# The first stage of a one-core transformer block in a fixed order, with half the first modulation sums and each second row's product moved to TensorE

## The chip, the cores and the metric

The kernel runs on one core of one Trainium2 chip. A core has TensorE (PE; its weight loads are listed as PEld), VectorE (DVE), ScalarE (ACT), GpSimd (POOL) and SyncE (SP), which here only issues transfers. Each engine executes its own list of instructions in order. The metric is the device time of one execution in microseconds (us). One execution was also recorded by the hardware profiler; all rows of the trace come from that one.

## The reference

One decoder block on 1024 tokens of width 1024, batch 1, all in float32. Only its head matters here:

```python
mod = einsum('bd,de->be', silu(c), w_ada) + b_ada            # w_ada: 1024 x 6144
shift1, scale1, gate1, shift2, scale2, gate2 = split(mod, 6)
h = rms_norm(x, norm1_w) * (1 + scale1) + shift1
proj = einsum('btd,de->bte', h, w_in)                        # w_in: 1024 x 7184
q, k, v, r, a_lr, su, sv, g_a, g_b = split(proj, ...)
```

From `proj` come a chunked gated linear attention (its decay from `a_lr`, rank 16), a spatial gating unit, two sigmoid gates and one output projection; after that a mixer that picks 16 of 16384 single-neuron experts for each of 8 heads and token, and a final norm.

## The kernel before

The tokens are done in two halves of 512. In a half the normed and modulated input is kept transposed: row k (of 8) holds 128 features by 512 tokens. To keep float32 accuracy at TensorE's quicker rate, each operand is split into a rounded part and its rest (`hTh`, `hTl` for the input, `wh`, `wl` for a weight tile), and three products are summed: high by high, high by rest, rest by high. A *group* is one 1024x512 slice of `w_in`: 8 rows, and for each row four blocks of 128 tokens, so 12 products into four PSUM tiles `mm`. The weight tiles `wt` (128x512, four buffers) are loaded by SP; ScalarE rounds them (L1253), VectorE takes the rest (L1254). The 14 groups, the output projection and the query projection follow one another.

The *first stage* is what must happen before and during the first group (`G_V0`) of the first half:

- `x_first`: eight loads of x, squares on ScalarE (L1196), pair sums on VectorE (L1198), a product with `ones` (L1199), the norm of each token `rstd`, and its spread over the partitions by a product (L1165) into `rrow` (L1167).
- `ada_cols(kp)`, four times: a quarter of the columns of shift1 and scale1. Each of 8 rows of `w_ada` (a tile 128x512, two rows to a buffer, eight buffers) is scaled by a column of silu(c) and added up, in two chains of four rows: the first by ScalarE (L1124), three by VectorE (L1126). Eight one-column products with `ones` (L1132) add up the partitions, VectorE adds the bias into `mod` (L1134) and makes `scol` = (1 + scale) * norm weight (L1136). A quarter serves two rows k.
- `h_first(k)`: `xt` times `rrow` on VectorE (L1224); the modulated row twice on ScalarE, rounded into `hTh` (L1211) and whole into `xt` (L1213); the rest `hTl` on VectorE (L1216).
- after the group, 24 products of 16 rows (`gaux`) for the decay input `a_lr`, with `walr_h` and `walr_l`.

The text issues these in the order of the program, and a list scheduler that simulates a timeline reorders each engine's list; only places under `issue_after` are held. Later, queues of generators interleave other work with the groups: the remaining rows of `w_ada` (L1103 to L1108, four rows of 1024 columns), the routing and the gathered experts, all of whose order the scheduler also sets.

## Time and profile before

| | |
|---|---|
| median of 3 runs | 1452.01 us (1451.76 to 1453.45) |
| the profiled execution | 1450.17 us, span 1448.4 us |
| mean granted TensorE clock | 0.971 |
| TensorE busy | 1348.1 us, 93% of the span |
| VectorE busy | 1091.7 us, 75% |
| ScalarE busy | 737.9 us, 51% |
| DMA, mean | 238 GB/s |

The span is the time from the profile's first event to its last; the execution's own time is 1.8 us more. In a row of the timeline the first number is the start in us, the second the length, then engine, line, operation, result<-operands; a number behind x says how many neighbours were merged. A row of the groups gives the count, the busy time with the mean length in ns, and the idle time before it with what ended it. An f32 product with f32 on both sides leaves two records in the trace, and each record of TensorE is longer than the spacing to the next one, since products overlap.

### The profile page before, as it was taken

To read this page: it belongs to the slowest core of one execution; us is meant where nothing else is said; L and a number is where in the kernel's file an instruction comes from. 1 tells how busy PE (TensorE), PEld (TensorE's weight loads), DVE (VectorE), ACT (ScalarE), POOL (GpSimd) and SP (SyncE) were. 2 spreads that over 40 slices of the span, in tenths; PEclk is the share of its full clock that TensorE was granted. 3 is DMA by queue.
4 is the path that set the end of the run, shared out by engine and by line. 5 is a ranking of instruction groups with operands and counts; after the bars stand their busy time and mean duration, and the time that the engine had idled before them with its cause. 6 is when DMAs were issued, how large, how long until landed. Compare 5 with 4: busy or idle time off the path is not lost.

```text
span 1448.4 us, 19642 instructions
## 1 busy us (share of the span) xinstructions
PE 1348.1 (93%) x6004; PEld 1039.6 (72%) x6004; DVE 1091.7 (75%) x3114; ACT 737.9 (51%) x1611; POOL 278.7 (19%) x275
## 2 busy tenths in 40 slices
PE   3999999999999889997989999999988999789996
PEld 2778877888888778776868787887766886445553
DVE  6584768443468669988879888778889877799775
ACT  4454333333255456474534677556645555556542
POOL 0100001000000011422442133221111024443331
PEclk8899999999999999998999999999998999999999
DMA  9552454322258484757587689796687669987984
GB/s 321 184 214 95 170 184 161 105 95 88 88 171 280 160 291 168 265 177 275 194 308 263 222 325 343 286 354 216 219 324 264 227 216 356 355 347 303 419 331 166
DMA packets 120836, 345.00 MB, mean 238 GB/s; under 512 B 15033, under 2 KB 24505, under 8 KB 108690
## 3 DMA queue, kind: packets, MB, share of 16 engines
q0 software_dynamic: 32064, 165.95, 30.7%
q1 hardware_dynamic: 70992, 133.20, 26.8%
q10 hardware_dynamic: 17666, 44.53, 8.5%
q8 instruction: 48, 0.79, 0.2%
q14 instruction: 66, 0.54, 0.1%
HBM read 319.40 MB, written 24.23 MB: 237 GB/s over the span
## 4 chain that ended last, share of the span: by engine, by line
PE 41%; DMA 8%; DVE 7%; issue 5%; ACT 4%; POOL 1%; ACTq 0%; DVEq 0%; POOLq 0%
PE acc L606 7%; PE mm L181 6%; PE mm L182 6%; PE mm L184 6%; DMA uv<-in_tab_dram,ix 4%; PE mm L187 3%; PE mm L188 3%; PE mm L189 3%; PE aux L1655 2%; PE hps L578 1%; DMA wt<-in_w_inp_dram 1%; PE hps L579 1%; DVE wl L1254 1%; DVE uv L580 1%; DMA xb<-in_x_dram 1%
## 5 line engine op out<-in xcount | busy, mean ns | idle before, releaser
L1253 ACT ACTIVATE wh<-wt 128x512 fp32r<-128x512 f32 x368 | 228.2, 628 | 322.9 <-PE mm L182 133.5
L1254 DVE TENSOR_TENSOR wl<-wt,wh 128x512 fp32r<-128x512 f32 x368 | 247.7, 685 | 137.1 <-ACT wh L1253 73.2
L181 PE MATMUL mm<-wh,hTh 128*128 128x512 f32 x672 | 265.9, 398 | 3.1 <-ACT wh L1253 3.1
L182 PE MATMUL mm<-wh,hTl 128*128 128x512 f32 x672 | 263.8, 395 | 0.0
L184 PE MATMUL mm<-wl,hTh 128*128 128x512 f32 x672 | 207.6, 394 | 0.0
L181 PEld LDWEIGHTS mm<-wh,hTh 128*128 128x128 f32 x672 | 127.1, 189 | 35.0 <-ACT wh L1253 4.8
L182 PEld LDWEIGHTS mm<-wh,hTl 128*128 128x128 f32 x672 | 126.9, 189 | 27.1 <-issue 1.0
L184 PEld LDWEIGHTS mm<-wl,hTh 128*128 128x128 f32 x672 | 125.6, 188 | 27.0 <-DVE wl L1254 0.6
L525 POOL DMA_INDIRECT uv<-in_tab_dram,ix x74 | 80.4, 1086 | 262.9 <-ACT ix L557 178.3
L187 PE MATMUL mm<-wh,hTh 128*128 128x512 f32 x224 | 90.5, 413 | 8.4 <-ACT hTh L1211 5.5
L182 PE MATMUL mm<-hTl,wh 128*128 128x512 f32 x240 | 96.5, 402 | 0.0
L181 PE MATMUL mm<-hTh,wh 128*128 128x512 f32 x240 | 95.9, 400 | 0.0
L580 DVE SCALAR_TENSOR_TENSOR uv<-uv,hps 128x512 f32<-128x512 f32 x112 | 74.8, 679 | 24.5 <-DMA uv<-in_tab_dram,ix 16.8
L188 PE MATMUL mm<-wl,hTh 128*128 128x512 f32 x224 | 89.1, 398 | 0.1
L189 PE MATMUL mm<-wh,hTl 128*128 128x512 f32 x224 | 88.4, 397 | 0.0
L187 PE MATMUL mm<-hTh,wh 128*128 128x256 f32 (+1 forms) x208 | 71.6, 346 | 10.7 <-DVE q L1383 7.6
L188 PE MATMUL mm<-hTl,wh 128*128 128x256 f32 (+1 forms) x208 | 69.8, 337 | 3.0 <-DVE hTl L173 3.0
L184 PE MATMUL mm<-hTh,wl 128*128 128x512 f32 x240 | 71.4, 398 | 0.0
L752 POOL DMA_INDIRECT uvd<-in_down_dram,dix x32 | 37.1, 1159 | 177.8 <-DVE cidx L353 40.0
L618 DVE SCALAR_TENSOR_TENSOR vl<-uv,r,vh 128x512 fp32r<-128x512 f32 x84 | 61.3, 745 | 10.6 <-ACT vh L617 7.7
L189 PE MATMUL mm<-hTh,wl 128*128 128x256 f32 (+1 forms) x208 | 68.9, 337 | 0.0
L578 PE MATMUL hps<-hh,E 128*128 128x512 f32 x132 | 62.4, 473 | 4.5 <-DVE uv L580 3.6
(938 smaller groups left out, 2875.3 us busy)
## 6 DMA issues: line engine op xcount, KB each, us to landing
wt<-in_w_inp_dram SPq DMA_DIRECT2D x224, 256.0 KB, 3.5
wt<-in_w_qp_dram SPq DMA_DIRECT2D x80, 256.0 KB, 3.0
wada<-in_w_ada_dram SPq DMA_DIRECT2D x32, 512.0 KB, 4.8
wt<-in_w_outp_dram SPq DMA_DIRECT2D x64, 256.0 KB, 3.5
wada<-in_w_ada_dram SPq DMA_DIRECT2D x32, 256.0 KB, 5.8
s_d<-so ACTq DMA_DIRECT2D x28, 256.0 KB, 5.3
xr<-in_x_dram ACTq DMA_DIRECT2D x8, 512.0 KB, 6.5
x_d<-x ACTq DMA_DIRECT2D x8, 512.0 KB, 4.4
```

The source lines that it names most:

```text
L181: nc.tensor.matmul(ps, lh, rh, start=False, stop=False)
L182: nc.tensor.matmul(ps, *((lh, rl) if feat else (ll, rh)), start=False, stop=False)
L184: nc.tensor.matmul(ps, *((ll, rh) if feat else (lh, rl)), start=False, stop=False)
L187: nc.tensor.matmul(ps, lh, rh, start=first, stop=False)
L188: nc.tensor.matmul(ps, lh, rl, start=False, stop=False)
L189: return nc.tensor.matmul(ps, ll, rh, start=False, stop=last).ins
L525: nc.gpsimd.indirect_dma_start(out=dst[:], out_offset=None, in_=src, in_offset=off)
L578: nc.tensor.matmul(hps, Ej, hh[:, sl], start=True, stop=False)
L580: nc.vector.scalar_tensor_tensor(uv[0][:, sl], uv[0][:, sl], 1.0, hps, op0=OP.mult, op1=OP.mult, accum_out=r[:, 2 + n:3 + n])
L606: ins = nc.tensor.matmul(acc[:, sl], W, v[:, sl], start=first, stop=last).ins
L1253: nc.scalar.activation(wh, wt, AF.Identity)
L1254: nc.vector.tensor_tensor(wl, wt, wh.bitcast(F32), op=OP.subtract)
```

## The change

The first stage gets a function of its own, `first_group`, whose instructions go out through `put`: each is held behind the one that the same engine issued before it, so the order of the text is the order on each engine.

- Squares are added up one by one on VectorE into one tile; four one-column products give the row sums. Five products of 256 columns, with no use for the result (`warm`), stand between the squares on TensorE.
- Of the first quarter of the modulation, rows 1, 3, 5 and 7 of `w_ada` (`DIRECT`) no longer go through the chain: TensorE multiplies them with the column of silu(c) itself, four one-column products a row. The other quarters have one chain of 8 rows, not two of four: 1 step on ScalarE and 7 on VectorE, and four closing products, not eight.
- `xt` times `rrow` is done two rows at a time, when a quarter comes up, not eight rows ahead.
- Rows 1, 3, 5 and 7 of the group are multiplied whole, in f32 (`whole`): four products, no `wh` and `wl`. The even rows keep the split form. `hTl` is still made for all, for the decay products, which now stand between the rows of the group.
- The loads of `walr`, `wal`, `balt`, `keyst` and `sgub` go from ScalarE's queue to SP's: `walr` behind the first two weight tiles, the others at the end of the stage.
- `weights_ahead` holds its splits behind the last modulation (`hlast`), and the second half's rows are modulated on VectorE as before.

The diff, cut to its core:

```diff
-HA = (range(8), ())
+DIRECT = ((1, 3, 5, 7), (), (), ())
+WARM = (2, 3, 4, 5, 6)
...
-        for src, hi, lo in ((walr, walr_h, walr_l), (wal, wal_h, wal_l)):
-            nc.vector.tensor_copy(hi, src)
-            nc.vector.tensor_tensor(lo, src, hi.bitcast(F32), op=OP.subtract)
+        tail = {}
+
+        def put(eng, fn, *args, **kw):
+            with tc.issue_after(tail[eng]) if eng in tail else nullcontext():
+                tail[eng] = getattr(getattr(nc, eng), fn)(*args, **kw).ins
+
+        def split_const(src, hi, lo):
+            put("vector", "tensor_copy", hi, src)
+            put("vector", "tensor_tensor", lo, src, hi.bitcast(F32), op=OP.subtract)
...
-        def ada_cols(kp):
...
+        class AdaCols:
+            def __init__(self, kp):
+                w2 = 2 * P
+                self.kp, self.direct = kp, DIRECT[kp]
+                self.acc = gl.tile([P, 2, w2], F32, name="adc", bufs=3)
...
+            def add(self, n):
+                for _ in range(n):
+                    q = self.chain.pop(0)
+                    if len(self.chain) + len(self.direct) == KD - 1:
+                        put("scalar", "activation", self.acc, self.wa[q], AF.Identity, scale=sc[:, q:q + 1])
                     else:
+                        put("vector", "scalar_tensor_tensor", self.acc, self.wa[q], sc[:, q:q + 1], self.acc,
+                            op0=OP.mult, op1=OP.add)
...
+            def product(self, src, rhs, first, last):
+                for c in range(2):
+                    for j in range(2):
+                        put("tensor", "matmul", self.ps[:, c, j:j + 1], src[:, c, j * P:(j + 1) * P], rhs,
+                            start=first and c == 0 and j == 0, stop=last and c == 1 and j == 1)
+
+            def products(self, qs):
+                for q in qs:
+                    self.product(self.wa[q], sc[:, q:q + 1], q == self.direct[0], False)
+
+            def close(self):
+                self.product(self.acc, ones[:, 0:1], not self.direct, True)
+
+            def store(self):
+                k = 2 * self.kp
+                put("vector", "tensor_tensor", mod.rearrange("p (c k) -> p c k", c=2)[:, :, k:k + 2], self.ps,
+                    badat.rearrange("p (c k) -> p c k", c=2)[:, :, k:k + 2], op=OP.add)
+                put("vector", "scalar_tensor_tensor", scol[:, k:k + 2], mod[:, KD + k:KD + k + 2], 1.0, n1t[:, k:k + 2],
+                    op0=OP.add, op1=OP.mult)
...
-        def x_first():
...
+        def first_group(src, evac, aps):
...
+            def fetch(kp):
+                st = AdaCols(kp)
+                for k in (2 * kp, 2 * kp + 1):
+                    wts[k] = wst_p.tile([P, 512], F32, name="wt")
+                    put("sync", "dma_start", wts[k], src[:, k, :])
+                return st
...
+            st = fetch(0)
+            put("sync", "dma_start", walr, w_alr)
+            acc = t2("sqa")
+            warm = gauxt([P, 256])
+            for k in range(KD):
+                sq = rowp.tile([P, HALF], F32, name="sq", tag="row") if k else acc
+                put("scalar", "activation", sq, xts[k], AF.Square)
+                if k in WARM:
+                    put("tensor", "matmul", warm, ones, sq[:, 0:256], start=True, stop=True)
+                if k:
+                    put("vector", "tensor_tensor", acc, acc, sq, op=OP.add)
+            sps = auxt([P, BH])
...
+                put("tensor", "matmul", sps[:, i:i + 1], acc[:, i * P:(i + 1) * P], ones[:, 0:1], start=i == 0,
+                    stop=i == BH - 1)
+            st.products(st.direct[:2])
+            st.add(2)
+            rstd = sm_p.tile([P, BH], F32, name="rstd")
...
+            st.add(1)
+            dg = t2("dg")
...
+            st.products(st.direct[2:])
+            rps = auxt([P, HALF])
+            put("tensor", "matmul", rps, ones, dg, start=True, stop=True)
+            rrow = t2("rrow")
+            put("scalar", "activation", rrow, rps, AF.Identity)
+            st.add(len(st.chain))
+            st.close()
+
+            def products(k, wh, wl):
+                for n in range(3):
+                    a, w = ((hTh, wh), (hTh, wl), (hTl, wh))[n]
+                    for i, cs in enumerate(cuts):
+                        put("tensor", "matmul", pss[i], a[:, k, cs], w, start=k == 0 and n == 0, stop=False)
+
+            def whole(k):
+                for i, cs in enumerate(cuts):
+                    put("tensor", "matmul", pss[i], xts[k][:, cs], wts[k], start=False, stop=k == KD - 1)
+
+            def low(k):
+                wh = wsp.tile([P, 512], F32R, name="wh")
+                wl = wsp.tile([P, 512], F32R, name="wl")
+                put("scalar", "activation", wh, wts[k], AF.Identity)
+                put("vector", "tensor_tensor", wl, wts[k], wh.bitcast(F32), op=OP.subtract)
+                return wh, wl
+
+            def scale_row(k):
+                put("vector", "tensor_tensor", xts[k], xts[k], rrow, op=OP.mult)
+
+            def modulate(dst, k):
+                put("scalar", "activation", dst, xts[k], AF.Identity, scale=scol[:, k:k + 1], bias=mod[:, k:k + 1])
+
+            def rest_of(k):
+                put("vector", "tensor_tensor", hTl[:, k], xts[k], hTh[:, k].bitcast(F32), op=OP.subtract)
+
+            def alpha(k):
+                for n, (a, w) in enumerate(((hTh, walr_h), (hTl, walr_h), (hTh, walr_l))):
+                    put("tensor", "matmul", aps, w[:, k], a[:, k], start=k == 0 and n == 0, stop=k == KD - 1 and n == 2)
+
+            whl = low(0)
+            scale_row(0)
+            for ka in range(0, KD, 2):
+                kb = ka + 1
+                st.store()
+                scale_row(kb)
+                st = fetch(kb // 2 + 1) if kb < KD - 1 else None
+                more = st.add if st else id
+                more(1)
+                for k in (ka, kb):
+                    modulate(hTh[:, k], k)
+                    modulate(xts[k], k)
+                for k in (ka, kb):
+                    more(1)
+                    rest_of(k)
+                if ka == 0:
+                    split_const(walr, walr_h, walr_l)
+                products(ka, *whl)
+                if st:
+                    st.add(len(st.chain))
+                    whl = low(kb + 1)
+                    scale_row(kb + 1)
+                    whole(kb)
+                    alpha(ka)
+                    st.close()
+                    alpha(kb)
+                else:
+                    alpha(ka)
+                    whole(kb)
+                    alpha(kb)
+            hlast[:] = [tail["scalar"], tail["vector"]]
+            for dst, src_ in ((wal, w_al), (balt, b_alT), (keyst, keysT), (sgub, sgu_bT)):
+                put("sync", "dma_start", dst, src_)
+            split_const(wal, wal_h, wal_l)
+            for i in range(4):
+                evac(i, pss[i])
+            return tail["tensor"]
...
-                nc.scalar.activation(wh, wt, AF.Identity)
-                nc.vector.tensor_tensor(wl, wt, wh.bitcast(F32), op=OP.subtract)
+                with tc.issue_after(hlast[0]):
+                    nc.scalar.activation(wh, wt, AF.Identity)
+                with tc.issue_after(hlast[1]):
+                    nc.vector.tensor_tensor(wl, wt, wh.bitcast(F32), op=OP.subtract)
...
-            group(w_inp[G_V0], ev_v(0), False, None if hf else h_first)
+            aps = gauxt([RANK, HALF])
+            if hf:
+                group(w_inp[G_V0], ev_v(0), False)
+                for k in range(KD):
+                    alr = mm3(aps, walr_h[:, k], walr_l[:, k], hTh[:, k], hTl[:, k], k == 0, k == KD - 1)
+            else:
+                alr = first_group(w_inp[G_V0], ev_v(0), aps)
```

What this does to the lists of the engines at the two places of which the prediction speaks (a row is a line, an operation, result<-operands and shape; x and a number is how many in a row; in the changed kernel all of the stage has line 1089, the line in `put`).

VectorE from the end of the row norms to the first products. `dg` is the diagonal from which the norm is spread, `xt` the input row, `wl` the rest of a weight tile, `adc` the chain of the modulation sums. Before:

```order
L1162 TENSOR_TENSOR dg<-ident,rstd 128x512
L1126 SCALAR_TENSOR_TENSOR adc<-wada,sc,adc 128x512
L1224 TENSOR_TENSOR xt<-xt,rrow 128x512 x8
L1254 TENSOR_TENSOR wl<-wt,wh 128x512 x2
L1134 TENSOR_TENSOR mod<-aux,badat 128x2x2
L1126 SCALAR_TENSOR_TENSOR adc<-wada,sc,adc 128x512 x2
L1136 SCALAR_TENSOR_TENSOR scol<-mod,n1t 128x2
```

Now:

```order
L1089 TENSOR_TENSOR dg<-ident,rstd 128x512
L1089 SCALAR_TENSOR_TENSOR adc<-wada,sc,adc 128x512
L1089 TENSOR_TENSOR wl<-wt,wh 128x512
L1089 TENSOR_TENSOR xt<-xt,rrow 128x512
L1089 TENSOR_TENSOR mod<-aux,badat 128x2x2
L1089 SCALAR_TENSOR_TENSOR scol<-mod,n1t 128x2
L1089 TENSOR_TENSOR xt<-xt,rrow 128x512
```

One scaling and one `wl` stand ahead of `mod`, where eight and two stood, and `scol` follows `mod` at once.

TensorE from its first matmul to the end of the first two rows. `aux` are the sums, `gaux` the warming and the decay products, `mm` the group. Before:

```order
L1199 MATMUL aux<-sq,ones 128x512 x4
L1165 MATMUL aux<-dg,ones 128x512
L1132 MATMUL aux<-ones,adc 128x1 x9
L187 MATMUL mm<-wh,hTh 128x512
L188 MATMUL mm<-wl,hTh 128x512
```

and, three more such pairs later:

```order
L187 MATMUL gaux<-hTh,walr_h 16x512
L1132 MATMUL aux<-ones,adc 128x1 x8
L189 MATMUL mm<-wh,hTl 128x512 x4
L181 MATMUL mm<-wh,hTh 128x512
L182 MATMUL mm<-wh,hTl 128x512
```

Now:

```order
L1089 MATMUL gaux<-sq,ones 128x256 x5
L1089 MATMUL aux<-ones,sqa 128x1 x4
L1089 MATMUL aux<-sc,wada 128x1 x16
L1089 MATMUL aux<-dg,ones 128x512
L1089 MATMUL aux<-ones,adc 128x1 x4
L1089 MATMUL mm<-wh,hTh 128x512 x4
L1089 MATMUL mm<-wl,hTh 128x512 x4
L1089 MATMUL mm<-wh,hTl 128x512 x4
L1089 MATMUL mm<-wt,xt 128x512 x4
L1089 MATMUL gaux<-hTh,walr_h 16x512
L1089 MATMUL gaux<-hTl,walr_h 16x512
L1089 MATMUL gaux<-hTh,walr_l 16x512
```

```order
L1089 MATMUL aux<-ones,adc 128x1 x4
L1089 MATMUL gaux<-hTh,walr_h 16x512
L1089 MATMUL gaux<-hTl,walr_h 16x512
L1089 MATMUL gaux<-hTh,walr_l 16x512
L1089 MATMUL mm<-wh,hTh 128x512 x4
```

The 16 products of w_ada stand ahead of the spread of the norm; the whole products of the second row stand ahead of the next quarter's closing products (the second fence follows the first without a gap), and the decay products have moved between the rows.

More of the change, by code (lines that the diff above doesn't have):

```diff
@@ L126, in block_kernel @@
     n1t = load_const("n1t", n1T, [P, KD])
-    keyst = load_const("keyst", keysT, [P, 2, NK])
+    keyst = const.tile([P, 2, NK], F32, name="keyst")
     ebase = const.tile([P, NT], F32, name="ebase")
@@ L1186, in x_prep, with h_split @@
             return xts
-        def x_first():
-            xts = []
-            sps = auxt([P, BH, P])
+        hlast = []
+        def h_split(k):
+            xt = xts[k]
+            nc.scalar.activation(hTh[:, k], xt, AF.Identity, scale=scol[:, k:k + 1], bias=mod[:, k:k + 1])
+            nc.vector.tensor_scalar(xt, xt, scol[:, k:k + 1], mod[:, k:k + 1], op0=OP.mult, op1=OP.add)
+            nc.vector.tensor_tensor(hTl[:, k], xt, hTh[:, k].bitcast(F32), op=OP.subtract)
+        def first_group(src, evac, aps):
+            pss = [mm.tile([P, 512], F32, name="mm", tag="mm") for _ in range(4)]
+            cuts = [slice(i * P, (i + 1) * P) for i in range(4)]
+            xts, wts = [], {}
+            del plan[:KD]
+            def fetch(kp):
[4 more added lines that the diff above has]
+                return st
@@ L1191, in x_first @@
             for k in range(0, KD, 2):
                 xt = v4.tile([P, 2, HALF], F32, name="xt", tag="v4")
[L1193 removed]
                 for kk in range(2):
[L1195 to L1196 removed]
+                    put("sync", "dma_start", xt[:, kk], xT[(k + kk) * P:(k + kk + 1) * P, 0:HALF])
                     xts.append(xt[:, kk])
[L1198 removed]
@@ L1276, in stream, with group @@
                     evac(i, pss[i])
[L1278 removed]
+            def group(src, evac, feat, post=None):
                 def body(k, ws, pss):
@@ L1329, in block_kernel @@
                     qa.add(ada_row(c, r))
-            aps = gauxt([RANK, HALF])
-            for k in range(KD):
-                alr = mm3(aps, walr_h[:, k], walr_l[:, k], hTh[:, k], hTl[:, k], k == 0, k == KD - 1)
             alh = t2("alh", F32R)
```

81 lines of the change are left out of this document (19 added, 62 removed).

## The prediction

> **What bounds the kernel now.** I read the busy times first, then the stretches of the first 75 us, then the timeline of each engine there.
>
> ```profile
> span 1448.4 us, 19642 instructions
> PE 1348.1 (93%) x6004; PEld 1039.6 (72%) x6004; DVE 1091.7 (75%) x3114; ACT 737.9 (51%) x1611; POOL 278.7 (19%) x275
> ```
>
> TensorE is busy for 1348 of 1448 us, so time is won where it idles or runs slowly. The stretches (start:end, length, busy time of PE, PEld, DVE, ACT, POOL, granted TensorE clock, DMA share, GB/s) show both in the first stage:
>
> ```profile
> 10.00:15.00 5.00, 2.78 (x4) 1.24 (x5) 3.90 (x8) 2.85 (x12) 0.00 (x0) 1.00 0.99 328
> 25.00:30.00 5.00, 3.31 (x16) 3.23 (x16) 4.65 (x8) 2.69 (x5) 0.00 (x0) 0.50 1.10 352
> 30.00:35.00 5.00, 1.17 (x3) 0.98 (x4) 5.00 (x11) 3.30 (x5) 0.00 (x0) 0.50 1.08 360
> 35.00:40.00 5.00, 5.00 (x19) 4.14 (x18) 2.98 (x5) 0.90 (x2) 0.00 (x0) 0.50 1.09 368
> 45.00:50.00 5.00, 5.00 (x23) 3.50 (x21) 2.74 (x5) 0.87 (x2) 0.00 (x0) 0.87 0.25 88
> 50.00:55.00 5.00, 5.00 (x29) 4.35 (x29) 3.50 (x7) 4.01 (x6) 0.00 (x0) 1.00 0.06 21
> ```
>
> VectorE is full where TensorE waits (25 to 35), the clock is at half until about 46, and the DMA engines are full until 40. The timeline (start, length, instruction, and in brackets what ended the idle time) names the wait:
>
> ```profile
> 24.48 3.84 PE L1132 MATMUL aux<-ones,adc 128*128 128x1 f32 x18
> 25.35 4.91 DVE L1224 TENSOR_TENSOR xt<-xt,rrow 128x512 f32<-128x512 f32 x8 [2.13 <-ACT rrow L1167]
> 31.38 0.16 DVE L1134 TENSOR_TENSOR mod<-aux,badat 128x4 f32<-128x4 f32 x1
> 32.77 0.15 DVE L1136 SCALAR_TENSOR_TENSOR scol<-mod,n1t 128x2 f32<-128x2 f32 x1
> 33.83 0.80 PE L187 MATMUL mm<-wh,hTh 128*128 128x512 f32 x1 [5.51 <-ACT hTh L1211]
> 51.21 0.16 DVE L1134 TENSOR_TENSOR mod<-aux,badat 128x4 f32<-128x4 f32 x1 [3.01 <-PE aux L1132]
> 59.87 0.17 DVE L1134 TENSOR_TENSOR mod<-aux,badat 128x4 f32<-128x4 f32 x1 [2.98 <-PE aux L1132]
> 72.33 0.39 PE L187 MATMUL mm<-wh,hTh 128*128 128x512 f32 x1
> ```
>
> The first quarter's sums leave TensorE at 28.3 (24.48 + 3.84), but `mod` is stored at 31.4 behind the eight scalings, and `scol` 1.4 later behind two more steps. First product 33.8. The first and the last `mod` stand 28.5 us apart, three quarters of 9.5 each. The second group of weights starts at 72.3 and from there TensorE hardly stops; so the question is when that second group starts in the changed kernel.
>
> **Term 1, the way to the first quarter.** The rows that price it:
>
> ```profile
> 0.79 6.55 SPq L1195 DMA_DIRECT2D xt<-in_xT_dram  x8
> xt<-in_xT_dram SPq DMA_DIRECT2D x8, 256.0 KB, 3.3
> 16.10 0.72 ACT L1124 ACTIVATE adc<-wada,sc 128x512 f32<-128x512 f32 x1 [0.62 <-DMA wada<-in_w_ada_dram]
> 19.12 0.72 ACT L1124 ACTIVATE adc<-wada,sc 128x512 f32<-128x512 f32 x1 [2.29 <-DMA wada<-in_w_ada_dram]
> 22.61 2.08 PE L1165 MATMUL aux<-dg,ones 128*128 128x512 f32 x2 [5.06 <-DVE dg L1162]
> L1196 ACT ACTIVATE sq<-xt 128x512 f32<-128x512 f32 x8 | 4.4, 617 | 4.0 <-DMA keyst<-in_keysT_dram 3.4 <-PE aux L1199 0.6
> ```
>
> The last of eight transfers of x is issued at about 7.0 and lands 3.3 to 4.3 later: 10.5 here. Square 0.62 and add 0.69: 11.8. From there TensorE runs its fixed row. A one-column product in full f32 is two records; at half clock 18 take 3.84, or 0.21 to 0.23 each. Four sums for the row norms, 8 records, 1.8: 13.6. Four rows of w_ada straight from the load, 32 records, 7.0: 20.6; their data are there in time, since the third pair of rows landed by 16.1 and the next quarter's first at 19.1. The product that spreads the row norm over the partitions, 2.0: 22.6 (the norm itself is ready by then, from VectorE and GpSimd). The closing four, 1.8: 24.4. The scaling and the `wl` ahead of `mod` on VectorE end by 23.9 (22.6 + 0.6 for `rrow` + 0.7). `mod` and `scol`: 24.7. So **the first store moves from 31.4 to 24.4**, 7.0 earlier. Removing five constant loads from ScalarE's queue costs nothing: their consumers now come tens of us later, and if one were late VectorE would wait at the `wal_h` cast, with the `wl` of the second group behind it.
>
> **Term 2, one quarter of the loop.** Durations at full and at half clock:
>
> ```profile
> 34.42 0.63 PE L188 MATMUL mm<-wl,hTh 128*128 128x512 f32 x1
> 34.85 0.63 PE L187 MATMUL mm<-wh,hTh 128*128 128x512 f32 x1
> 61.62 0.39 PE L181 MATMUL mm<-wh,hTh 128*128 128x512 f32 x1
> 61.85 0.39 PE L182 MATMUL mm<-wh,hTl 128*128 128x512 f32 x1
> 544.00 1.02 PE L1165 MATMUL aux<-dg,ones 128*128 128x512 f32 x2
> 49.34 1.98 PEld L1132 LDWEIGHTS aux<-ones,adc 128*128 128x128 f32 x16
> L1126 DVE SCALAR_TENSOR_TENSOR adc<-wada,sc,adc 128x512 f32<-128x512 f32 x24 | 17.3, 748 | 1.2 <-ACT adc L1124 0.9 <-DMA wada<-in_w_ada_dram 0.2
> L1216 DVE TENSOR_TENSOR hTl<-xt,hTh 128x512 fp32r<-128x512 f32 x8 | 5.2, 687 | 0.0
> L1211 ACT ACTIVATE hTh<-xt,mod,scol 128x512 fp32r<-128x512 f32 x8 | 6.1, 804 | 4.4 <-DVE scol L1136 4.4
> ```
>
> A split product starts every 0.23 at full clock and every 0.43 at half. The whole product (f32 on both sides) is the form of L1165: two records, about 0.86 at full clock less the drain. Its price is certain in kind: four take 3.4, where the twelve split ones of that row took 2.7, so TensorE pays 0.7 more for each second row; ScalarE saves a `wh` (0.63) and VectorE a `wl` (0.69).
>
> From `mod` to the first product is 1.75 before (59.87 to 61.62); say 1.5, as `adc` no longer stands between. Then, in TensorE's order: 12 split products 2.7, 4 whole 3.4, three alpha products 0.7, four closing ones (8 records) 1.0. That is 9.3 until the next `mod`. VectorE's own row is 7 x 0.75 + 5 x 0.69 + 0.3 = 9.0 by these means (back to back less: the eight scalings above took 0.61 each). Its sums are done two steps before its end, near 7.7, plus what two waits for ScalarE's four modulations of 0.80 add: about when TensorE reaches the closing products, at 8.3. I take **9.4** a quarter: no gain on the 9.5 of before, since one row of sums more on VectorE (seven steps, not six) and the whole products on TensorE eat what the dropped `wl` saves. If the closing products wait for VectorE, it is 9.0 + 1.0 = 10; over three quarters 1.8 more.
>
> The first quarter begins at half clock. How long? Before, products ran densely from 41.1 and the clock rose within 45 to 50:
>
> ```profile
> 41.10 2.05 PE L189 MATMUL mm<-wh,hTl 128*128 128x512 f32 x4
> 45.94 0.55 PE L182 MATMUL mm<-wh,hTl 128*128 128x512 f32 x1
> 46.32 1.09 PE L184 MATMUL mm<-wl,hTh 128*128 128x512 f32 x4
> ```
>
> The spacing shrinks at 46.3: 5.2 us of dense work. From the first product of the stage (33.83) it was 12.5, with one-column products in between. I take 5.2, the nearest in kind, half of it lost: 2.6, so the first quarter costs 12.0. With 12.5 nearly the whole quarter would run at half clock: 1.5 + 12 x 0.43 + 4 x 1.7 + 3 x 0.43 + 1.8 = 16.5, so 7.1 lost instead of 2.6; that end, 1448.5, stays in the range. [...]
>
> **Term 3, the end of the stage.** After the last `mod`: 1.5 + 2.7 + 0.7 + 3.4 + 0.7 = 9.0. Before, it was 12.5 (59.87 to 72.33), because work of the quarter ahead was still queued.
>
> **Sum.** 24.4 + 12.0 + 9.4 + 9.4 + 9.0 = 64.2 against 72.3: **8.1 us earlier**. The execution shown took 1450.17 us with a span of 1448.4; the median of the three runs is 1452.01, 1.8 above it. Of the 50 us stretches from 100 to 450 only two show TensorE idle:
>
> ```profile
> 150.00:200.00 50.00, 48.48 (x238) 39.46 (x237) 35.88 (x55) 18.31 (x45) 0.00 (x0) 1.00 0.55 189
> 400.00:450.00 50.00, 48.74 (x234) 40.13 (x233) 38.29 (x60) 26.26 (x45) 1.46 (x2) 1.00 0.62 212
> ```
>
> That is under 3 us, and what idles waits for work that moves along, so the shift passes through. I forecast 1452.0 - 8.1 = **1444.0**.
>
> **Rivals.** *The clock rises early and stays (0.16).* The five warming products (two records each at 256 columns, 0.43 a record, 4.3 us) may raise the clock near 10 us, and the one-column products might hold it. For it: the clock read 1.00 from 10 to 20. Against: after the burst that ended at 17.6 it was down at 22.6. Then records cost 0.12 instead of 0.22; the first `mod` is bound by landing (the last rows at about 17.6) and comes at 20.7; no half-clock quarter: 20.7 + 28.2 + 9.0 = 57.9, 1437.6. [...]
>
> *Loads come late (0.10).* Eight buffers hold two quarters of w_ada, and of the four weight tiles every second one is now freed only by its whole product.
>
> ```profile
> 32.22 1.92 SPq L1122 DMA_DIRECT2D wada<-in_w_ada_dram  x4
> wada<-in_w_ada_dram SPq DMA_DIRECT2D x32, 256.0 KB, 5.8
> ```
>
> The last quarter of w_ada was issued by 34 and landed by 40. Now it stands behind weight tile 5, which waits for the whole product of row 1, about 35; landing to about 44, needed from 45.8. Each us beyond that slack is lost; 4 lost gives 1448.
>
> *The later part takes it back (0.14).* The scheduler orders the second half anew: one gather of 128x2048 becomes two of 128x1024, and routed and dense work interleave differently.
>
> ```profile
> PE mm L187 <- DVE q L1383: 7.6, 1, 7.6
> PE acc L606 <- ACT rd L536: 6.9, 1, 6.9
> ```
>
> One new wait of this size cancels the gain: 1452. Nothing says which way; such an order can also win 3.
>
> *Slower: the clock stays at half through the loop (0.07).* A whole row costs 6.8 there. Three quarters of 16.5 as above and an end of 1.5 + 5.2 + 1.3 + 6.8 + 1.3 = 16.1 give 24.4 + 49.5 + 16.1 = 90.0, 17.7 later than before: 1469.7. It decides once two quarters are cold (8.1 - 4.5 - 7.1 is below nothing). For it: before, it took until 46.3. Against: with gaps of under 2 us between quarters it read 1.00 from 50 on.
>
> *The fixed orders are not what is issued* (0.03): the listed rows follow the text; then about 1452.
>
> **Numbers.** The forecast has 0.50, with its own range 1440 to 1448. About 0.2%, 2.9 us, is what a measurement of this kernel can tell from no change. Faster: 0.50 x 0.97 + 0.16 + 0.10 x 0.6 + 0.14 x 0.3 + 0.02 from the rest of the order's luck = 0.77, same 0.14, slower 0.09. Range 1436 to 1451: it holds the early clock and most of the late loads, and leaves out the cold loop and half of the later losses.
>
> **What would show it.** First `mod` near 24 and first split product near 26; clock at half from about 15 to 30; four stores 9 to 10 apart but for the first, 12; second group from 64. A first `mod` near 21 shows the early clock; VectorE idle for `wada` in the third quarter shows late loads; clock 0.50 beyond 40 the slower case. A second group at 64 with an end that has not moved shows the later part.

## The result, and the profile after

The changed kernel took 1445.05 us in the median of 14 runs (1437.18 to 1451.39), the kernel before 1452.74 beside it (14 runs, 1449.02 to 1468.71). The ratio is 0.9947, with a 95% interval of 0.9925 to 0.9969: 7.7 us faster, between 4.5 and 10.9. Forecast were 1444.0 us and a gain of 8.1. The profiled execution, though, is the longest of its 14 (1451.39 us), and its span is longer than that of before (1448.4). The page's first rows of the changed kernel:

```profile
span 1449.7 us, 19609 instructions
PE 1354.9 (93%) x5998; PEld 1039.5 (72%) x5998; DVE 1091.3 (75%) x3105; ACT 731.4 (50%) x1603; POOL 282.8 (20%) x276
```

So the whole time of one execution can't show the gain here, and the first stage has to be read by itself. Its timeline (TensorE and VectorE):

```profile
11.41 1.87 PE L1089 MATMUL aux<-ones,sqa 128*128 128x1 f32 x8
13.13 6.96 PE L1089 MATMUL aux<-sc,wada 128*128 128x1 f32 x32
15.06 0.68 DVE L1089 TENSOR_TENSOR dg<-ident,rstd 128x512 f32<-128x512 f32 x1
19.96 2.05 PE L1089 MATMUL aux<-dg,ones 128*128 128x512 f32 x2
23.20 0.69 DVE L1089 TENSOR_TENSOR wl<-wt,wh 128x512 fp32r<-128x512 f32 x1 [6.54 <-ACT wh L1089]
24.41 0.15 DVE L1089 TENSOR_TENSOR mod<-aux,badat 128x4 f32<-128x4 f32 x1
25.66 2.07 PE L1089 MATMUL mm<-wh,hTh 128*128 128x512 f32 x4 [2.15 <-ACT hTh L1089]
30.50 3.60 PE L1089 MATMUL mm<-wt,xt 128*128 128x512 f32 x8
35.62 0.16 DVE L1089 TENSOR_TENSOR mod<-aux,badat 128x4 f32<-128x4 f32 x1 [1.40 <-PE aux L1089]
44.98 0.16 DVE L1089 TENSOR_TENSOR mod<-aux,badat 128x4 f32<-128x4 f32 x1
54.33 0.16 DVE L1089 TENSOR_TENSOR mod<-aux,badat 128x4 f32<-128x4 f32 x1
63.27 0.39 PE L188 MATMUL mm<-wh,hTh 128*128 128x512 f32 x1
```

First `mod` 24.41, quarters of 11.2, 9.4 and 9.4, and 8.9 to the second group: it starts 9.1 us earlier than before (72.33). One thing is odd: `dg` is ready at 15.7, but the product that spreads it runs at 19.96, behind 32 one-column records, and VectorE idles 6.54 us around it.

A second profile of the same program shows another first quarter:

```profile
11.41 1.24 PE L1089 MATMUL aux<-ones,sqa 128*128 128x1 f32 x8 [0.32 <-DVE sqa L1089]
12.51 4.49 PE L1089 MATMUL aux<-sc,wada 128*128 128x1 f32 x32
21.31 0.15 DVE L1089 TENSOR_TENSOR mod<-aux,badat 128x4 f32<-128x4 f32 x1
59.51 0.39 PE L188 MATMUL mm<-wh,hTh 128*128 128x512 f32 x1
```

The same 32 records take 4.49 us, not 6.96, and the second group starts at 59.51. Three questions follow: which parts of the change earn the 9 to 13 us, what decides between 59.5 and 63.3, and why the whole time follows the stage so loosely. Of the 9.1 us in the first profile, 7.0 lie ahead of the first `mod` and 3.5 behind the last one, and the three quarters between take back 1.4 (29.9 against 28.5).

### The profile page after: what moved, and what is told of

Same layout as the page of the kernel before. It is cut to its first block, busy times and chain, and to the rows that moved or that the text cites. A ratio compares the mean times of both kernels' runs of the same rounds, so it can differ in the third digit from the quotient of the medians.

```text
span 1449.7 us, 19609 instructions
## 1 busy us (share of the span) xinstructions
PE 1354.9 (93%) x5998; PEld 1039.5 (72%) x5998; DVE 1091.3 (75%) x3105; ACT 731.4 (50%) x1603; POOL 282.8 (20%) x276
## 4 chain that ended last, share of the span: by engine, by line
PE 35%; DMA 10%; DVE 9%; issue 6%; ACT 5%; POOL 2%; ACTq 0%; SPq 0%; DVEq 0%; POOLq 0%
PE acc L607 6%; PE mm L182 5%; PE mm L183 5%; PE mm L185 5%; DMA uv<-in_tab_dram,ix 2%; PE mm L188 2%; PE mm L190 2%; PE mm L189 2%; PE aux L1766 1%; DMA uvd<-in_down_dram,dix 1%; PE hps L579 1%; DMA uv<-in_tab_dram,dix 1%; DVE uv L581 1%; DVE wl L1364 1%; PE hps L580 1%
## 5 line engine op out<-in xcount | busy, mean ns | idle before, releaser
L1362 ACT ACTIVATE wh<-wt 128x512 fp32r<-128x512 f32 x360 | 223.2, 628 | 306.7 <-PE mm L183 118.2
L1364 DVE TENSOR_TENSOR wl<-wt,wh 128x512 fp32r<-128x512 f32 x360 | 241.4, 683 | 142.4 <-ACT wh L1362 70.5
L182 PE MATMUL mm<-wh,hTh 128*128 128x512 f32 x648 | 257.0, 397 | 4.1 <-ACT wh L1362 4.1
L183 PE MATMUL mm<-wh,hTl 128*128 128x512 f32 x648 | 254.4, 393 | 0.0
L185 PE MATMUL mm<-wl,hTh 128*128 128x512 f32 x648 | 202.9, 396 | 0.3 <-DVE wl L1364 0.2
L182 PEld LDWEIGHTS mm<-wh,hTh 128*128 128x128 f32 x648 | 122.0, 188 | 34.0 <-ACT wh L1362 6.0
L183 PEld LDWEIGHTS mm<-wh,hTl 128*128 128x128 f32 x648 | 121.9, 188 | 26.0 <-issue 1.0
L185 PEld LDWEIGHTS mm<-wl,hTh 128*128 128x128 f32 x648 | 120.9, 188 | 27.0 <-issue 1.1
L526 POOL DMA_INDIRECT uv<-in_tab_dram,ix x73 | 77.2, 1058 | 241.2 <-ACT ix L558 145.2
L188 PE MATMUL mm<-wh,hTh 128*128 128x512 f32 x216 | 86.1, 410 | 4.0 <-ACT sg L1598 2.8
L189 PE MATMUL mm<-wl,hTh 128*128 128x512 f32 x216 | 85.7, 397 | 0.0
L190 PE MATMUL mm<-wh,hTl 128*128 128x512 f32 x216 | 85.4, 396 | 0.0
```

The costliest lines, as they stand in the source:

```text
L182: nc.tensor.matmul(ps, lh, rh, start=False, stop=False)
L183: nc.tensor.matmul(ps, *((lh, rl) if feat else (ll, rh)), start=False, stop=False)
L185: nc.tensor.matmul(ps, *((ll, rh) if feat else (lh, rl)), start=False, stop=False)
L188: nc.tensor.matmul(ps, lh, rh, start=first, stop=False)
L189: nc.tensor.matmul(ps, lh, rl, start=False, stop=False)
L190: return nc.tensor.matmul(ps, ll, rh, start=False, stop=last).ins
```

## The experiments

Each is the changed kernel with the edit named, timed in turn with the kernel before. None leaves out or changes a part of what is returned; the products that some add or drop have no reader. The row sums, which wait for the last loads of x, start up to 1.2 us apart between executions (11.39 to 12.64), so places in the stage are also given from the start of the row sums (11.41 above): the second group stands 51.9 behind it in the first profile, 48.1 in the second. All columns behind the ratio are in us.

| run | ratio to before (95%) | row sums | first `mod` | second group | the same, behind the row sums | last x to last `so` |
|---|---|---|---|---|---|---|
| before | 1 | | 31.4 | 72.3 | | 155.4 |
| changed, first | 0.9947 (0.9925 to 0.9969) | 11.41 | 24.4 | 63.3 | 51.9 | 156.7 |
| changed, again | 0.9944 (0.9912 to 0.9976) | 11.41 | 21.3 | 59.5 | 48.1 | 152.9 |
| 1 scalings first | 0.9966 (0.9943 to 0.9989) | 12.40 | 29.6 | 68.5 | 56.1 | 155.7 |
| 2 no direct rows | 0.9913 (0.9886 to 0.9940) | 12.64 | 22.8 | 61.6 | 49.0 | 154.0 |
| 2 once more | 0.9898 (0.9863 to 0.9933) | 11.39 | 21.1 | 59.9 | 48.5 | 154.6 |
| 3 no warming | 0.9954 (0.9929 to 0.9979) | 11.39 | 24.4 | 63.0 | 51.6 | 153.1 |
| 4 odd rows split | 1.0017 (0.9993 to 1.0041) | 11.48 | 23.4 | 62.6 | 51.1 | 162.1 |
| 5 some more products | 0.9952 (0.9925 to 0.9979) | 12.64 | 22.3 | 60.9 | 48.2 | 153.7 |
| 6 warming from 1 us | 0.9931 (0.9903 to 0.9958) | 12.22 | 21.6 | 59.8 | 47.6 | 154.5 |
| 7 scalings first, other list | 1.0032 (0.9996 to 1.0069) | 11.85 | 26.1 | 65.2 | 53.3 | 165.6 |
| 8 dense start, row 5 direct | 0.9927 (0.9900 to 0.9953) | 11.41 | 19.2 | 56.7 | 45.2 | 163.7 |
| 8 dense start, none direct | 0.9922 (0.9899 to 0.9944) | 11.64 | 20.3 | 57.7 | 46.1 | 156.7 |
| 8 dense start, rows 1 and 5 | 0.9892 (0.9863 to 0.9921) | 11.81 | 23.6 | 62.8 | 51.0 | 150.5 |

The last column is read far behind the stage: from the second half's last x (L1688) to its last router scores `so` (L1768). The *list* of a run is the order in which its engines' instructions are issued behind the stage; the scheduler draws it anew for each program.

**1. All scalings ahead of the first store.**

```diff
-            scale_row(0)
+            for k in range(KD):
+                scale_row(k)
...
-                scale_row(kb)
...
-                    scale_row(kb + 1)
```

> All eight row scalings stand again ahead of the first store of `mod` on VectorE; the rest is the changed kernel, and nothing is left out. In the changed kernel VectorE runs `wl` and one scaling between `rrow` and `mod`, and TensorE's closing products end at 23.5, 0.9 before `mod` at 24.4. Theory (VectorE's queue ahead of `mod` is what the quarter-by-quarter order saves): seven more scalings at 0.61 each are 4.3 us, less the one that stood right behind the store; `mod` near 28.5, second group near 67 (63.3 + 4), as the later quarters have 0.6 less on VectorE each but wait for TensorE anyway. Rival (TensorE's one-column work alone sets the first store): `mod` stays within 0.5 of 24.4 and the second group within 1 of 63.3. In the whole time theory +2 to +5 us, rival no change; the place in the stage decides, not the whole time.

VectorE's timeline of this run:

```profile
24.80 4.90 DVE L1089 TENSOR_TENSOR xt<-xt,rrow 128x512 f32<-128x512 f32 x8
29.62 0.15 DVE L1089 TENSOR_TENSOR mod<-aux,badat 128x4 f32<-128x4 f32 x1
```

`mod` stands 17.2 behind the row sums and not 13.0: 4.2 later, and the second group 4.2 later too. The order of VectorE's queue earned that much of the stage. But the median, 1444.0, is not 2 to 5 us longer; run 2 shows why.

**2. No direct rows.**

```diff
-DIRECT = ((1, 3, 5, 7), (), (), ())
+DIRECT = ((), (), (), ())
```

> No row of w_ada goes straight to TensorE: all eight rows of the first quarter are summed on VectorE (and ScalarE's part), nothing is left out. In the changed kernel VectorE stands idle for 6.5 us (16.65 to 23.2) while TensorE runs 32 one-column records, 7.0 us, at 0.22 each, and the product that spreads the norm waits behind them although its input `dg` is there at 15.7. Theory (the direct products are on the path): the spread runs at 15.8, four more sums of 0.75 end with the last rows' landing near 19, closing 1.8, `mod` at 20.7 to 21.2, 3.4 earlier; second group near 59.8 (59 to 61). Rival (the direct products relieve a full VectorE): `mod` 2.7 later, near 27, second group near 66. Whole time: theory 2 to 5 us less than the changed kernel, rival 2 to 3 more.

Its timeline:

```profile
12.64 1.87 PE L1089 MATMUL aux<-ones,sqa 128*128 128x1 f32 x8 [0.30 <-DVE sqa L1089]
17.07 2.08 PE L1089 MATMUL aux<-dg,ones 128*128 128x512 f32 x2 [2.56 <-DVE dg L1089]
20.97 1.84 PE L1089 MATMUL aux<-ones,adc 128*128 128x1 f32 x8 [1.83 <-DVE adc L1089]
22.84 0.16 DVE L1089 TENSOR_TENSOR mod<-aux,badat 128x4 f32<-128x4 f32 x1 [0.82 <-PE aux L1089]
```

The spread now waits for `dg` alone. `mod` stands 10.2 behind the row sums, 2.8 earlier than in the first profile of the changed kernel (expected 3.4). The rival is out: VectorE had the room. The median is 1437.8, 7.2 under the changed kernel where 2 to 5 were expected. Of the change, the move of half the sums to TensorE costs time when the records take 0.22 each. Where they take 0.14 (the second profile, 9.9 behind) it costs next to nothing: without direct rows and with the row sums at full clock, too, it is 9.7 (this run once more, below).

Runs 1 and 2 also answer a part of the third question. Taken by operation and tile, their traces have nearly the same list: of VectorE's 3016 instructions behind the stage 2993 stand in the same order, of ScalarE's 1554 all but 9, while some 450 of VectorE's stand elsewhere than in the changed kernel. Between these two the whole time does follow the stage: second groups at 68.5 and 61.6, medians 1444.0 and 1437.8, the intervals just apart. So run 1 did lose what its stage lost; it lost it against run 2, whose list it shares, and not against the changed kernel, which has another.

**3. No warming products.**

```diff
-WARM = (2, 3, 4, 5, 6)
+WARM = ()
```

> The five warming products (10 records, 4.64 us, whose result nobody reads) are left out; what the kernel returns is computed as before. Theory (they do not raise the clock: a one-column record costs 0.22 behind them and a split product 0.43 until 29.5): first `mod` at 24.4, the split products at 0.43 until near 29.5, second group 63.3, all within 0.5. [...] Rival 2 (they do harm, in the way of the sums): second group earlier by up to 1.

```profile
11.39 1.87 PE L1089 MATMUL aux<-ones,sqa 128*128 128x1 f32 x8 [11.39 <-DVE sqa L1089]
13.12 6.96 PE L1089 MATMUL aux<-sc,wada 128*128 128x1 f32 x32
63.01 0.39 PE L188 MATMUL mm<-wh,hTh 128*128 128x512 f32 x1
```

The stage is, to within 0.3, that of the first profile of the changed kernel. Alone this would say that warming does nothing; runs 4 and 7 and the second profile of the changed kernel, all with warming, show it at work.

**4. Odd rows split, not whole.**

```diff
-                    whole(kb)
+                    products(kb, *whlb)
...
```

> Each second row is split into two parts as the first one is (twelve products per row, one more `wh` on ScalarE and one more `wl` on VectorE a quarter) and not multiplied whole; nothing is left out. In the changed kernel VectorE's last sum of a quarter ends at 43.77 and TensorE's closing products start at 43.92: the two engines are level. Theory (level engines, either binds): TensorE has 0.7 less a quarter but VectorE 0.6 to 0.7 more, and VectorE is waited for; three quarters 0.5 to 0.6 longer each, the last end 0.7 shorter: second group 64 to 65.2. Rival (TensorE's queue alone sets a quarter): four times 0.7 less, second group near 60.5. A third (whole products free the wrong buffers, fetching later): stalls on w_ada go away, which the changed kernel does not show.

The third and fourth closing sums now wait, and the quarters around them are 9.9 long (44.50 to 54.36), not 9.4:

```profile
42.92 1.02 PE L1089 MATMUL aux<-ones,adc 128*128 128x1 f32 x8 [0.61 <-DVE adc L1089]
44.50 0.15 DVE L1089 TENSOR_TENSOR mod<-aux,badat 128x4 f32<-128x4 f32 x1
54.36 0.15 DVE L1089 TENSOR_TENSOR mod<-aux,badat 128x4 f32<-128x4 f32 x1
62.56 0.39 PE L188 MATMUL mm<-wh,hTh 128*128 128x512 f32 x1
```

The first quarter is 11.3, the end 8.2 instead of 8.9: from the first `mod` to the second group 39.2, against 38.9. So the engines are level, as the first theory had it; whole rows are worth 0.3 us. The second group itself, at 62.6, lies under the expected 64 to 65.2, because the first `mod` came 1.0 earlier. Yet this kernel took 1452.25, 7 us more than the changed one.

This run also shows the clock. The granted clock (the column with 0.84 and 0.96, 1 for full speed) in stretches of the split-rows run and of the second profile of the changed kernel:

```profile
10.00:15.00 5.00, 4.14 (x28) 3.72 (x26) 3.10 (x6) 0.89 (x2) 1.02 (x1) 0.84 1.10 360
30.00:35.00 5.00, 5.00 (x27) 3.65 (x25) 4.05 (x9) 0.00 (x0) 0.00 (x0) 0.96 1.09 355
```

```profile
15.00:20.00 5.00, 5.00 (x20) 3.97 (x21) 1.20 (x2) 1.05 (x3) 0.00 (x0) 0.52 1.09 352
25.00:30.00 5.00, 5.00 (x17) 2.84 (x15) 4.82 (x9) 1.16 (x2) 0.00 (x0) 0.95 1.10 351
```

and of the kernel before:

```profile
20.00:25.00 5.00, 2.39 (x6) 1.36 (x6) 3.21 (x5) 0.28 (x1) 0.38 (x1) 0.74 1.09 360
```

The stretches between these read 0.50. So a stretch of 5 us at 0.84 holds 1.6 us at half: the clock fell at 13.4 and (0.96) rose at 30.4, 17.0 apart, each place good to 0.05. In the second profile it fell at 15.2 and rose at 25.5: 10.3. Before, it fell at 22.4 and rose at 46.3: 23.9. The same reading gives 13.7 in run 5 and in run 2 once more, 17.1 in run 7, and 6.8, 3.4 and 3.4 one behind the other in run 6. The shortest is 3.4, and the others are 2, 3, 4, 5 and 7 times as long; what sets these distances no run shows. The clock also fell while TensorE was busy. One-column products were not enough to hold it: in the second profile it fell at 15.2, and TensorE had run nothing but an unbroken row of them since 11.4.

Five warming products (4.64 us in both profiles of the changed kernel) raised the clock in the second and not in the first: the row sums take 1.05 to 1.37 in five of the eight profiles that have five or six of them and no more, 1.86 or 1.87 in three. What made the difference no run shows, but it decides between 59.5 and 63.3: with the clock up the first `mod` is 3.1 earlier and the first quarter 10.6 long, not 11.2.

**5 and 6. More products without a reader.** Run 5 is run 2 (no direct rows) with one more warming product and five products in gaps; run 6 has also ten products of `ones` by `ones`, which wait for no load.

```diff
-DIRECT = ((1, 3, 5, 7), (), (), ())
-WARM = (2, 3, 4, 5, 6)
+DIRECT = ((), (), (), ())
+WARM = (1, 2, 3, 4, 5, 6)
...
+            for _ in range(10):                       # run 6 alone
+                put("tensor", "matmul", warm[:, 0:P], ones, ones, start=True, stop=True)
...
+            hold(3)                                   # behind the row sums
...
+            hold(2)                                   # behind the closing sums
```

> As the run without direct products (all eight rows of the first quarter on VectorE; first `mod` 22.84, second group 61.59), with one more warming product ahead and five products whose result nobody reads: three behind the row sums, two behind the closing sums of the first quarter. What the kernel returns is computed as before. The order of the later part is that of the changed kernel. Theory (TensorE's clock is up from the start if it has dense work from 6.5 us on, and falls only behind a stretch of about 3.3 us without it, as in the run with split odd rows, where sums cost 0.13 each at 11.5 and 0.23 from 14 on): sums 1.05 and not 1.87, spread 1.0 and not 2.08, a split product 0.23 from the first, first quarter 9.4 and not 11.1: second group at 57 to 58.5, whole time 4 to 6 us under the changed kernel. Rival (six warming products are too few, the clock stays half until 3.9 us into the first quarter): the products without a reader are in the way, second group 61.5 to 63.

> The same with ten more products without a reader, of `ones` by `ones` (128 columns), which wait for no load and so start near 1.2 us, when `ones` is filled. They take about 4.6 us at half clock (two records of 0.23 each), so TensorE has 10 us of dense work until the row sums, instead of 5. What the kernel returns is computed as before. [...] Rival (one-column sums and the gaps around them let the clock fall again before the first quarter): sums at 0.13, split products at 0.43 for 3.9 us, second group 60 to 61.5.

Neither theory was met in run 5: row sums 1.37 (the clock fell among them, at 13.2: 0.82 from 10 to 15, and 1.5 us behind the last warming products, which ran from 10.32 to 11.67, where the theory has 3.3), spread 2.07, second group between the two ranges; the median, 1444.3, is not 4 to 6 us under the changed kernel. Run 6:

```profile
5.99 2.63 PE L1089 MATMUL gaux<-sq,ones 128*128 128x256 f32 x8 [0.47 <-ACT sq L1089]
9.90 1.33 PE L1089 MATMUL gaux<-sq,ones 128*128 128x256 f32 x4 [1.28 <-ACT sq L1089]
12.22 1.87 PE L1089 MATMUL aux<-ones,sqa 128*128 128x1 f32 x8 [0.99 <-DVE sqa L1089]
16.65 2.07 PE L1089 MATMUL aux<-dg,ones 128*128 128x512 f32 x2
20.55 1.02 PE L1089 MATMUL aux<-ones,adc 128*128 128x1 f32 x8 [1.83 <-DVE adc L1089]
22.87 2.08 PE L1089 MATMUL mm<-wh,hTh 128*128 128x512 f32 x4
```

The clock rose in the row at 5.99 (2.63 for eight records, 3.78 in run 2), but two gaps (1.28 and 0.99) lie ahead of the row sums, and these are at half clock again (1.87); the closing sums are at full, the first split products at half. It rose three times and fell twice (at 12.0 and 22.2: 0.70 from 10 to 15, 0.72 from 20 to 25). The second group came at 59.8. The rival holds in its main point, that the clock falls again; its row sums at full clock were wrong, and the second group is 0.2 under its range.

**7. Scalings first, with another list behind the stage.** Run 1 with one more warming product (run 1's own edit isn't shown again).

```diff
-WARM = (2, 3, 4, 5, 6)
+WARM = (1, 2, 3, 4, 5, 6)
```

> The run with all eight scalings ahead of the first store, plus one more warming product. On the chip that adds one product where TensorE waits for the next square (0.46), and the stage is that of the scale-first run: first `mod` about 17.2 behind the start of the row sums, second group about 56.1 behind it. But the scheduler's list for everything behind the stage comes out another (3294 rows of 5287 on TensorE differ from the changed kernel's list, where the scale-first run differs in 1874). Theory (the list of the later part is worth several us by itself): second group within 1 of the scale-first run, but the whole time 3 us or more away from its 1444. Rival (the whole time follows the second group): the same 1444 within 3.

The second group came 3.3 us earlier than in run 1, outside the expected 1, since the clock was up (32 direct records in 4.82). The whole time was 1458.4 against 1444.0 all the same; the intervals, 0.9943 to 0.9989 and 0.9996 to 1.0069, lie apart. What differs is the scheduler's list of the later part. Where it shows, in the rows of the second half's last x and last `so` (after the colon: shortest, median and longest ns; first and last start) of run 1,

```profile
L1688 DVE TENSOR_TENSOR x<-mm,g1row x16: 677/682/692, 432.8 to 1092.6; 128x512 f32<-128x512 f32 x16
L1768 ACT ACTIVATE so<-aux x32: 575/597/603, 475.5 to 1248.3; 128x512 f32<-128x512 f32 x32
```

and of run 7:

```profile
L1688 DVE TENSOR_TENSOR x<-mm,g1row x16: 680/688/692, 429.4 to 1098.6; 128x512 f32<-128x512 f32 x16
L1768 ACT ACTIVATE so<-aux x32: 577/597/601, 475.5 to 1264.2; 128x512 f32<-128x512 f32 x32
```

From the one to the other are 155.7 us in run 1 and 165.6 in run 7. The changed kernel and runs 3, 5 and 6, which share one list behind the stage, have 152.9 to 156.7; run 2 and its repeat, with another list, 154.0 and 154.6; the two that lost their gain, 4 and 7, have 162.1 and 165.6. Another 9.4 us lie between the first x and the last (669.2 in run 7, 659.8 in run 1), less the 3.4 by which run 7 led at the first. So the theory is borne out in its main point. TensorE is busy for 148.2 of the 155.7 us in run 1 and for 152.1 of the 165.6 in run 7, so 6.0 of the 9.9 us are idle time; the mean granted clock of the whole profiled execution is 0.983 in run 1 and 0.967 in run 7. The list costs waits and clock together. Which placement in it does so is open: no single wait of TensorE is that long.

**The changed kernel once more.**

> The changed kernel once more, as the measure for the runs that share its later order (no warming, held clock, warming from 1 us). All theories expect its median near 1445 and a second group near 63.3, within 1.7; it shows how far two executions of one program differ behind the stage. Its first profile took 1451.4, the slowest of its runs; if that is chance, this one is shorter by several us with the same second group.

It took 1443.36 in the median, as expected. Its profiled execution took 1437.21, with the span 14.2 us under the first; 3.8 of that are the stage. A second group within 1.7 of 63.3 was expected, and it came at 59.5: one program has two values.

**8. A dense start.** From 1.1 us to the first split product TensorE gets work: 32 products of `ones` by `ones`, then products without a reader behind the row sums and around the closing sums; the spread goes ahead of the direct rows. Three choices of direct rows, with three, six and two products without a reader ahead of the closing sums.

```diff
-DIRECT = ((1, 3, 5, 7), (), (), ())
-WARM = (2, 3, 4, 5, 6)
+DIRECT = ((5,), (), (), ())                           # or none, or (1, 5)
+WARM = ()
...
+            for _ in range(32):
+                put("tensor", "matmul", warm[:, 0:P], ones, ones, start=True, stop=True)
...
```

> TensorE is kept dense from 1.1 us to the first split product: 32 products of `ones` by `ones` (128 columns, no reader) from 1.1 to near 11, four products of 256 columns behind the row sums, three ahead of and three behind the closing sums; of the first quarter's rows only row 5 goes straight to TensorE, behind the spread. What the kernel returns is computed as before. [...] Its later order is a new one, worth -6 to +14 by the runs so far.

> The same with no direct row and six products without a reader between spread and closing sums (2.6 us at full clock, which VectorE's sums take anyway). Theory: `mod` 0.6 later than with row 5 direct, as VectorE has one sum of 0.75 more ahead; second group 45.6 to 46.6 behind the start of the row sums. [...] The later order is again another, so the whole times of the two may differ by several us though their second groups stand 0.6 apart.

> The same with rows 1 and 5 direct, behind the spread, two products without a reader behind them; its later order is the nearest of the three to that of the changed kernel (912 rows of difference on TensorE). [...] Whole time 1438 to 1442.

Timeline of the first:

```profile
1.10 9.02 PE L1089 MATMUL gaux<-ones 128*128 128x128 f32 x64 [1.10 <-DVE ones L112]
11.41 1.05 PE L1089 MATMUL aux<-ones,sqa 128*128 128x1 f32 x8 [1.28 <-DVE sqa L1089]
15.05 1.13 PE L1089 MATMUL aux<-dg,ones 128*128 128x512 f32 x2 [0.75 <-DVE dg L1089]
19.19 0.16 DVE L1089 TENSOR_TENSOR mod<-aux,badat 128x4 f32<-128x4 f32 x1
20.45 1.20 PE L1089 MATMUL mm<-wh,hTh 128*128 128x512 f32 x4
56.65 0.39 PE L188 MATMUL mm<-wh,hTh 128*128 128x512 f32 x1
```

No record at half clock from the row sums on, the first `mod` 7.8 and the second group 45.2 behind them; without direct rows 8.7 and 46.1, with the second group within the expected 45.6 to 46.6 and the first `mod` 0.9 later than with row 5 direct, not 0.6. These are the two shortest stages of all. With rows 1 and 5 direct the clock was not held: behind a gap of 1.86 ahead of the spread, and among 2.59 us of direct records, it fell at 18.4 (0.84 from 15 to 20), and the second group came at 62.8, 51.0 behind. Its whole time, 1440.5, lies in the expected 1438 to 1442 all the same. It even has the lowest ratio, 0.9892, and the one with the best stage has 163.7 in the last column and 0.9927; their intervals overlap. What the lists give or take makes up for 6 us of stage. The best stage has a list close to that of run 4 (all but some 200 of VectorE's 3016 instructions in the same order), and both have over 160 in the last column.

**2 once more.**

> The kernel without direct products once more. It was 1437.84 with a second group at 61.59, while the run with the same rows and a second group at 60.87 took 1444.34 in the changed kernel's later order. Theory (its later order is better by about 6 us): 1436 to 1440 again, 0.991 of the kernel before. Rival (a lucky session): near 1443, 0.994.

0.9898 and 1439.0: the good time of run 2 came again, in the same list and in the expected 1436 to 1440. Run 5, also without direct rows but in the changed kernel's list, had its second group at 60.9 and took 1444.3; by these medians the list of run 2 is the better one by 5 to 6 us, though the intervals of run 5 and of the two touch. In that list and without direct rows the kernel is 4 to 7 us under the changed one by the medians (1437.8 and 1439.0 against 1445.1 and 1443.4); the ratios' intervals still touch. With rows 1 and 5 and a dense start (0.9892, 0.9863 to 0.9921) the interval lies just below that of the first measurement of the changed kernel (from 0.9925), but not below that of the second.

## Why the prediction was right

**Term 1, the first store at 24.4.** 24.41, with each row on the way a little early: row sums to 13.3 (forecast 13.6), direct rows to 20.1 (20.6), spread to 22.0 (22.6), closing sums to 23.5 (24.4). But `mod` then waits 0.9 for VectorE, which the step had done by 23.9:

```profile
22.05 0.60 ACT L1089 ACTIVATE rrow<-aux 128x512 f32<-128x512 f32 x1 [9.95 <-PE aux L1089]
22.55 0.62 ACT L1089 ACTIVATE wh<-wt 128x512 fp32r<-128x512 f32 x1
23.81 0.68 DVE L1089 TENSOR_TENSOR xt<-xt,rrow 128x512 f32<-128x512 f32 x1
```

ScalarE makes `wh` behind `rrow`, and `wl` (at 23.20 above) waits for `wh`. From the end of the spread to `mod` lie four operations, 2.4 us; the step counted 1.3. So the last wait was named wrongly, VectorE's `wl` and scaling and not TensorE's closing sums (in the second profile, too, these end 0.9 ahead of `mod`), and 24.4 was met to the tenth by luck: the spread came 0.6 early, VectorE's chain behind it was counted 1.1 too short, and 23.9 - 0.6 + 1.1 is where TensorE's row had been expected to end.

Also, 24.4 is one of two values. The step took half clock for all one-column records; with the clock up through two thirds of them it is 21.3. That case stood in the rival of the early clock, bound to one-column products that hold the clock, and to a second group at 57.9. What happens lies between: the warming can raise it, the one-column products let it fall within about 4 us of their start (11.4 to 15.2), and 59.5 comes out.

**Term 2.** The first quarter is 11.2, forecast 12.0. The mis-sized term is the dense work until the clock rises, taken at 5.2: the spacing changed between 29.24 and 30.50, 3.6 to 4.8 behind the first product at 25.66, and the quarter is 1.8 longer than the next one, not 2.6. Later quarters: 9.36 and 9.35 against 9.4. That the whole products eat what VectorE saves, and the two engines end level, is what run 4 shows.

**Term 3.** 8.9, forecast 9.0. The sum is 63.3 against 64.2: 9.1 earlier by this profile, 12.8 by the other. What earns it is shown in part: run 1 takes back 4.2 of the 7.0 us ahead of the first `mod`. The 3.5 us at the end (12.5 before, 8.9 now) are read from the two timelines; no run undoes them alone.

**The shift passes through.** This step failed in part. In the five profiles with the changed kernel's list the first x (L1688) starts 361.3 to 364.2 behind the second group, before it was 359.9 (432.2 less 72.33): 3.3 us of the gain are gone by then, in the mean. TensorE's waits between 64 and 340 us, in the first profile of the changed kernel,

```profile
PE gaux L1537 <- DVE at L1529: 2.9, 1, 2.9
PE mm L190 <- DVE wl L1364: 1.0, 1, 1.0
```

and before:

```profile
PE gaux L1426 <- DVE at L1418: 1.5, 1, 1.5
```

The wait for `wl` is new, in all five, and the wait for `at` is 0.1 to 1.4 longer. And the stretch from 150 to 200 now holds a piece at half clock, in four of the five:

```profile
150.00:200.00 50.00, 47.08 (x217) 37.84 (x216) 33.53 (x51) 19.13 (x48) 0.00 (x0) 0.97 0.53 174
```

Before it read 1.00; 0.03 of 50 us is 1.5 us. Profile by profile the three together leave 0.3 to 0.4 us unexplained: 3.9 of 4.3 in this one, and 1.1 of 1.4 in the one without the piece at half clock (run 6). Whether the clock fell because of the longer waits is not shown.

From the first x to the last, 663.6 to 671.4 stand against 663.5, from there to the last `so` 152.9 to 156.7 against 155.4, and to the end 193.4 to 195.7 against 197.3. In the mean of the five: -11.0 (stage) + 3.3 + 4.6 - 1.2 - 2.9 = -7.2, beside the measured 7.7. Of the kernel before there is one profile, so the middle terms may be chance. The forecast of 8.1 met the median partly by luck: a stage that is better than forecast met losses that it left out.

**The rivals.** *Loads come late*: no; SP does wait for the whole product, but in the loop TensorE waits for ScalarE's `hTh` alone, 0.6 a quarter. *The clock stays at half through the loop*: no, 0.23 a product from 30 on. *The orders are not what is issued*: the timeline follows the text. *The later part takes it back* was the rival nearest to the truth, and undersized: a single new wait was its price, with 3 us to win. Runs 1 and 7, one warming product apart, differ by 14 us, against the better stage, and the list is what else differs. By the sum above, the changed kernel came out 7.7 us ahead and not at 0 because its list is about as good as that of before, and nothing in the profile of before could tell that.

## What to carry to other kernels

Where a scheduler orders what follows, an edit of a few us at the head draws a new order for all the rest, and that draw can weigh more than the edit: judge the edit by its own stage, and compare whole times only between kernels that share a list, as runs 1 and 2 do. Ahead of a stage that depends on TensorE's clock, feed it dense products without a gap and without a wait for loads, from the first microsecond; 4.6 us of it raised the clock in some executions of one program and not in others, while 9 to 10 us from the first microsecond raised it in all three of run 8. Work that is moved to an idle engine still has to stand behind what the critical path needs there: 32 cheap records ahead of the spread cost 2.8 us.

## What the runs showed of the hardware

- One-column products did not hold TensorE's clock: it fell at 13.4 (run 4) and 15.2 (second profile of the changed kernel) during an unbroken row of them. A one-column f32 record cost 0.21 us at half clock and 0.11 at full: the eight row sums stand 1.72 ahead of the next record in the first profile of the changed kernel (11.41 to 13.13) and 0.91 in run 7 (11.85 to 12.76).
- A recorded fall of the clock and a rise next to it were 3.4 and 6.8 us apart (run 6), 10.3 (second profile of the changed kernel), 13.7 (run 5), 17.0 (run 4) and 23.9 (before): 1, 2, 3, 4, 5 and 7 times 3.4.
- A split product of 512 columns cost 0.24 us at full clock, a whole one in f32 0.76: in the first profile of the changed kernel twelve of the former take 2.85 (36.88 to 39.73), four of the latter 3.04 (30.50 to 33.54).
- The granted clock read 1.00 until its first recorded change, also where the spacing shows half clock: in the first profile of the changed kernel every stretch from 10 to 35 reads 1.00, yet the twelve split products take 4.8 us there (25.66 to 30.50) and 2.9 in the next quarter (36.88 to 39.73). The spacing is the better witness at the start of a program.
